# Hybrid GLA/NSA decoder layer on one core: 13 row sums in place of 18, full products for the top decay level, norm rows on ScalarE's queue

## Chip, cores and metric

The kernel runs on one core of a Trainium2 chip. The metric is the device time of one execution in microseconds. The time before is the median of three runs.

## The reference

One decoder layer for 256 tokens of width 2048, all in float32. `n = rms_norm(x)` goes through one input projection `w_in` (2048 x 5672). Four heads of gated linear attention (GLA) and eight query heads of a sparse attention (NSA: compressed, selected and window branches) read its parts. Both outputs go through `w_out` and are added to `x`. A SwiGLU network of inner width 5632 follows.

```python
h = x + concatenate([gla_out, nsa_out]) @ w_out
m = rms_norm(h, ffn_norm_g)
out = h + (silu(m @ w_gate) * (m @ w_up)) @ w_down
```

In GLA, the scores within a chunk are `sum_d q[t,d] k[s,d] exp(b[t,d] - b[s,d])` for `s <= t`, with `b` the running sum of a log gate.

## The kernel before

**Precision.** TensorE works on float32r numbers. Each operand is split into a high part (ScalarE: `hi`, L136, L623) and the rest (VectorE: `lo`, L137, L624), and a product is three matmuls: hi x hi, hi x lo, lo x hi, each 128x128 by 512 columns at most. Attention's small products are plain float32, which the profile shows as two matmul passes each.

**Stages.** `x` is turned (L209: transposes through the identity), scaled by the columns of `attn_norm_g` (L254, L256) and split. The gains come as 16 rows of 128 (L179) that a transpose turns into columns (L217, L218); L254 needs them. The ten projections (`proj`, L290; products at L282) follow each other, with weights loaded by 1 MB (L127) into three `raw` buffers on SP's queue. While they and the two halves of `w_out` run, `drive` (L97) hands out steps of attention from the queues `urgent` and `later`: `gla_decay`, `gla_scores`, `gla_out`, the NSA parts.

**GLA scores.** A 128x128 block of scores is put together from eight products, one for each level l of `LEVELS` (0, 1, 2, 4 ... 64). Level l gives the pairs (t, s) that lie in the two halves of one group of 2 l tokens. Seven of the eight products are full 128x128 ones (L567). At l = 64, where one quarter alone is wanted, the kernel multiplies 64 columns by 64 (L565). In both cases VectorE then copies that quarter alone (L574).

**Feed-forward in sevens.** The inner width is cut into 11 blocks f of 512 (`gate_up`, L1060). In each block the 2048 inputs are taken as 8 pairs of 128 rows, with 2 token tiles and the two matrices gate and up. Done plainly, a pair is 8 products of 128x128 by 512, that is 24 matmuls. Done by a seven-product scheme of Strassen's kind it is 7 products, 21 matmuls; these need four sums of token tiles (`forms`) and four sums of weight rows. The sums of weights are made on VectorE in the block itself (L1097 to L1099) and split as the weights are (ftwo<-g and ftwo<-fsum at L623 and L624); a pair in eight needs no sums. `FIRST7` says which pairs of block f go in seven: two in f = 0, four in f = 1, pairs 0 to 5 in f = 2 to 4, and all eight from `ALL7` = 5 on. `ORDER1` = (0,1,2,6,3,4,5,7) is the order of pairs for f below `ALL7`, `ORDER` = (0,...,7) from there on. After its last pair in seven, a block adds up the partial banks (L1125 to L1129). Then follows the down stage of the block before (96 matmuls at L282, weights `w_down` through L1040).

**Sums made ahead.** For some pairs, `sum_rows` (L1002) makes the four sums much earlier, while the projections run: it loads the pair's gate and up rows (two 512 KB requests on SP's queue, L1008), adds four times 128x512 on VectorE (L1013), and writes the two results to DRAM by GpSimd's queue (L1017). The block then loads one row of weights less and the sums (L1092), and VectorE makes none. `SUMS` lists these pairs: (2, 5, 7) for f = 5 to 10, 18 in all. They form the `background`: `drive` takes one step of it whenever `rate[0]` units of main work have gone by. The rates are 12, 30, 60, 18 and 14, in order of stage.

**Buffers.** In the feed-forward part weights go through three `fraw` buffers, split weights through four `ftwo`, sums through two `fsum`. SP's requests are issued in order, so one that waits for its buffer holds those behind it.

Of the kernel before, what the change touches and what calls it, by code (L numbers as in the profile page):

```python
# [15 lines left out]
P = 128  # L16
# [6 lines left out]
NFB = DFF // FB  # L23
# [13 lines left out]
def kernel(  # L37
# [4 lines left out]
    nc = tc.nc  # L42
    act, mm = nc.scalar.activation, nc.tensor.matmul
# [24 lines left out]
    def bank():  # L68
        n_tiles[0] += 1
        return pp.tile([P, 512], F32, tag="bank", name=f"bank_{n_tiles[0]}")  # L70

    def behind(op):

        return tc.issue_after(op.ins) if op is not None else nullcontext()
# [5 lines left out]
    urgent, later, background = [], [], []  # L80
# [11 lines left out]
    def drain(queue):  # L92
        while queue:
            for _ in queue.pop(0):
                pass
# [16 lines left out]
    count, rate = [0], [0]  # L112
# [55 lines left out]
    rows0, rows, rows2 = g1([P]), g1([P]), g1([P])  # L168
# [5 lines left out]
    for c in range(2):  # L174
        k = slice(2 * c, 2 * c + 2)
        nc.sync.dma_start(x_sb[0][:, :, c * 256:(c + 1) * 256], xv[:, :, c * 256:(c + 1) * 256])
        if c == 0:

            nc.sync.dma_start(rows0[0:16, :], attn_norm_g.rearrange("o (c p) -> (o c) p", p=P))  # L179
            for i in range(2):  # L180
                nc.scalar.dma_start(first[0][:, i], wi[i * P:(i + 1) * P, C_LR:C_LR + W0])
        else:
            nc.sync.dma_start(first[0][:, k], wi[2 * P:4 * P, C_LR:C_LR + W0].rearrange("(k p) w -> p k w", p=P))
# [308 lines left out]
    def ev_conv(ct, dst):  # L492
        def f(banks):
            urgent.append(conv(scaled(banks), ct, dst))
        return f

    def to_qk(dst):
        def f(pair, y):
            act(dst[:, 2 * pair:2 * pair + 2, :], y, AF.Silu)
            yield  # L500
        return f
# [54 lines left out]
    def gla_scores(h, b, res):  # L556
        tb = slice(b * P, (b + 1) * P)
        sc, e = g1([P]), dec[h // 2]
        for half in range(2):
            p = bank()  # L560
            for j in range(4):
                l = LEVELS[4 * half + j]
                u, w = (e[l][:, h % 2, tb],) * 2 if l else (kT[:, h, tb], qT[:, h, tb])
                if 2 * l == P:
                    mm(p[:l, j * P + l:(j + 1) * P], u[:, :l], w[:, l:], start=True, stop=True)  # L565
                else:
                    mm(p[:, j * P:(j + 1) * P], u, w, start=True, stop=True)  # L567
                yield
            for j in range(4):
                l, pl = LEVELS[4 * half + j], p[:, j * P:(j + 1) * P]  # L570
                if l == 0:
                    TT(sc, pl, lmask[:, 0, :], ALU.mult)
                elif 2 * l == P:
                    nc.vector.tensor_copy(sc[:l, l:], pl[:l, l:])  # L574
                else:
                    nc.vector.copy_predicated(sc, lmask[:, 4 * half + j, :].bitcast(mybir.dt.uint32), pl)
        res["s"] = sc
# [355 lines left out]
    PAIRS7, FIRST7 = tuple(range(8)), {0: (0, 2), 1: (0, 2, 4, 5)}  # L933

    EARLY7 = (0,1,2,3,4,5)

    ALL7 = 5
    FIRST7.update({f: (0,1,2,3,4,5) for f in range(2, ALL7)})


    OLD = (1, 3)
# [54 lines left out]
                pair_forms(2 * n + pair, v)  # L996


    SUMS = (2,5,7)
    row_sums = {}  # L1000

    def sum_rows(f, pair):  # L1002

        n_tiles[0] += 1
        gate, up = g4([2, 512]), g4([2, 512])
        for to, m in ((gate, w_gate), (up, w_up)):
            with behind(last["dma"]):
                nc.sync.dma_start(to, m[0][2 * pair * P:(2 * pair + 2) * P, f * FB:(f + 1) * FB].rearrange("(k p) w -> p k w", p=P))  # L1008
        for _ in range(3):
            yield True  # L1010
        for o, i in ((up[:, 0], up[:, 1]), (up[:, 1], gate[:, 1]), (gate[:, 1], up[:, 0]), (gate[:, 0], gate[:, 1])):
            with behind(last["d"]):
                TT(o, o, i, ALU.add)  # L1013
            yield True
        to = row_sums[f, pair] = [dp.tile([P, 2, 512], F32, name=f"sums{i}_{f}_{pair}") for i in range(2)]
        for part, a in zip(to, (up, gate)):
            nc.gpsimd.dma_start(part, a)  # L1017
        for _ in range(1):
            yield True
# [40 lines left out]
    def gate_up(fb):  # L1060
# [11 lines left out]

        order, sevens = (ORDER0, ORDER1, ORDER)[0 if fb == 0 else 1 if fb < ALL7 else 2], FIRST7.get(fb, PAIRS7)
        last7 = max(sevens, key=order.index)
# [117 lines left out]

    drive([proj(C_LR, ev_go(0), ((0, 256), (256, 272)), first_chunk)], 2)
    constants()
    background += [sum_rows(f, pair) for f in range(ALL7, NFB) for pair in SUMS]
    rate[0] = 12
    drive([proj(C_GO + 512, ev_go(1)), proj(0, ev_conv(0, to_qk(qT))), proj(512, ev_conv(4, to_qk(kT))),
           proj(1024, ev_conv(8, to_v(0))), proj(1536, ev_conv(12, to_v(1)))], 1.5)
    later.append(gla_mix())
    rate[0] = 30  # L1200
    drive([proj(C_KC, ev_kc), proj(C_KS, ev_kv(0)),
           proj(C_KW, ev_kv(1), ((0, 256), (256, 280))), proj(C_NQ, ev_nq(0))], 2.5)
    later.append(nsa_mix())
    rate[0] = 60
    drive([proj(C_NQ + 512, ev_nq(1))], 2.5)
    rate[0] = 18
    drive([w_out_half(0)], 2)
    drain(urgent)
    drain(later)
    rate[0] = 14  # L1210
    drive([w_out_half(1)], 6)

    for f in range(NFB):
# [39 lines left out]
```

## Time and profile before

| | |
|---|---|
| time, median of 3 runs | 1118.97 us (1118.44 to 1119.41) |
| profiled execution | 1119.94 us, its span 1118.2 us |
| instructions | 14700 |
| VectorE / ScalarE busy | 87% / 66% of the span |
| HBM read / written | 243.45 MB / 20.97 MB |

The span is what the trace covers of one execution. PE is TensorE's matmuls and PEld its weight loads, which overlap with PE; DVE is VectorE, ACT ScalarE, POOL GpSimd, SP the engine that issues most DMA requests. Names of tiles come without their numbers, so that `g` stands for many buffers. L1066 holds the products of `gate_up`, L282 those of projections, `w_out` and the down stages. Matmuls are pipelined: a busy time of PE counts the stretch from the first start to the last end, and the pace is read from the distance of starts.

### The profile page before, as it was taken

Reading aid. Unit: us, or ns where it says so; the run is one execution under the profiler, and the core shown is the slowest. Engines: PE = TensorE matmul, PEld = TensorE weight load, DVE = VectorE, ACT = ScalarE, POOL = GpSimd, SP = SyncE. Lnnn points to the kernel's source line nnn. Section 1 sums busy time; section 2 is a strip of 40 time slices with the busy share of each in tenths; the row PEclk is TensorE's granted clock in tenths of the full one; section 3 lists DMA queues with packets and bytes.
Section 4 is the critical chain, followed back from the end, with each engine's and each line's share of the span. In section 5 each row is a group of like instructions: output and inputs, shape, how many; then the busy total and the mean of one; then the engine's idle time right before and its main releaser. Section 6 shows DMA issues by size and latency. Waiting matters only on the chain.

```text
span 1118.2 us, 14700 instructions
## 1 busy us (share of the span) xinstructions
PE 1107.2 (99%) x5360; PEld 909.4 (81%) x5360; DVE 975.4 (87%) x1262; ACT 739.9 (66%) x1005; POOL 50.1 (4%) x97
## 2 busy tenths in 40 slices
PE   9999999999999999999999999999999999999998
PEld 8888887898778887887888888888878888888886
DVE  6678779988588889999899999899999999999981
ACT  6645557544575486657586676768686876868693
POOL 3110000111001001000000000000000000000000
PEclk9999999999999999999999999999999999999999
DMA  8999985475884686747465756767767768777772
GB/s 282 325 337 364 356 286 178 122 249 181 267 302 165 245 291 232 249 162 243 153 212 176 244 166 215 241 231 245 235 245 243 256 209 282 252 247 230 243 241 94
DMA packets 128338, 265.39 MB, mean 237 GB/s; under 512 B 6869, under 2 KB 9977, under 8 KB 128266
## 3 DMA queue, kind: packets, MB, share of 16 engines
q1 hardware_dynamic: 122794, 245.04, 64.8%
q0 software_dynamic: 5184, 18.88, 4.2%
q8 instruction: 42, 0.69, 0.2%
q10 hardware_dynamic: 288, 0.54, 0.2%
q14 instruction: 30, 0.25, 0.1%
HBM read 243.45 MB, written 20.97 MB: 236 GB/s over the span
## 4 chain that ended last, share of the span: by engine, by line
PE 90%; DVE 3%; DMA 3%; ACT 2%; issue 1%; POOL 0%; SPq 0%; ACTq 0%; POOLq 0%; DVEq 0%
PE bank L282 47%; PE bank L1066 36%; PE bank L209 3%; DMA raw<-in_w_out_dram 1%; PE bank L883 1%; PE bank L567 1%; DMA fraw<-in_w_down_dram 1%; DVE ftwo L624 1%; DVE lo L137 1%; ACT ftwo L623 1%; PE bank L821 1%; ACT hi L136 0%; DMA g<-in_attn_norm_g_dram 0%; PE bank L737 0%; POOL sm L212 0%
## 5 line engine op out<-in xcount | busy, mean ns | idle before, releaser
L1066 PE MATMUL bank<-ftwo,g 128*128 128x512 f32 x1848 | 431.6, 393 | 0.2 <-ACT ftwo L623 0.2
L1066 PEld LDWEIGHTS bank<-ftwo,g 128*128 128x128 f32 x1848 | 341.9, 188 | 77.1 <-DVE ftwo L624 3.1
L282 PE MATMUL bank<-hi,g 128*128 128x512 f32 (+2 forms) x1088 | 323.8, 377 | 0.0
L624 DVE TENSOR_TENSOR ftwo<-fraw,ftwo 128x1536 fp32r<-128x1536 f32 (+1 forms) x130 | 258.0, 1992 | 10.9 <-ACT ftwo L623 9.9
L282 PE MATMUL bank<-ftwo,g 128*128 128x512 f32 x1056 | 243.1, 390 | 0.7 <-ACT g L623 0.6
L623 ACT ACTIVATE ftwo<-fraw 128x1536 fp32r<-128x1536 f32 (+1 forms) x130 | 217.6, 1677 | 25.8 <-DMA fraw<-in_w_up_dram 13.5
L282 PEld LDWEIGHTS bank<-ftwo,g 128*128 128x128 f32 x1056 | 197.6, 188 | 43.4 <-ACT bank L1172 1.2
L282 PEld LDWEIGHTS bank<-hi,g 128*128 128x128 f32 x1088 | 192.8, 189 | 30.4 <-issue 1.0
L136 ACT ACTIVATE hi<-raw 128x1024 fp32r<-128x1024 f32 (+3 forms) x124 | 130.2, 1057 | 106.5 <-PE bank L282 64.6
L282 PE MATMUL bank<-lo,g 128*128 128x512 f32 (+3 forms) x544 | 195.3, 377 | 1.6 <-DVE lo L137 1.6
L137 DVE TENSOR_TENSOR lo<-raw,hi 128x1024 fp32r<-128x1024 f32 (+3 forms) x124 | 150.1, 1218 | 37.6 <-ACT hi L136 36.9
L623 ACT ACTIVATE ftwo<-g 128x1024 fp32r<-128x1024 f32 x72 | 76.2, 1059 | 75.2 <-DVE g L1097 59.8
L282 PEld LDWEIGHTS bank<-lo,g 128*128 128x128 f32 x544 | 98.7, 189 | 17.1 <-DVE lo L137 2.6
L624 DVE TENSOR_TENSOR ftwo<-g,ftwo 128x1024 fp32r<-128x1024 f32 x72 | 87.8, 1220 | 15.7 <-ACT ftwo L623 15.7
L1186 ACT COPY g<-bank 128x512 f32<-128x512 f32 (+1 forms) x96 | 51.4, 553 | 56.2 <-PE bank L282 54.1
L624 DVE TENSOR_TENSOR ftwo<-fsum,ftwo 128x1024 fp32r<-128x1024 f32 x72 | 87.8, 1220 | 0.4
L623 ACT ACTIVATE ftwo<-fsum 128x1024 fp32r<-128x1024 f32 x72 | 75.7, 1052 | 3.5 <-DVE fsum L1099 2.7
L1097 DVE TENSOR_TENSOR g<-fraw 128x1024 f32<-128x1024 f32 x54 | 65.3, 1219 | 0.3 <-issue 0.3
L1172 ACT COPY bank<-g 128x512 f32<-128x512 f32 x88 | 49.8, 593 | 12.4 <-DVE f L1128 10.7
L623 ACT ACTIVATE g<-bank 128x512 fp32r<-128x512 f32 (+1 forms) x50 | 29.0, 592 | 32.6 <-PE bank L209 22.2
L209 PE MATMUL bank<-ident,g 128*128 128x128 f32 (+2 forms) x214 | 37.5, 276 | 1.6 <-DMA g<-in_attn_norm_g_dram 1.3
L1099 DVE TENSOR_TENSOR fsum<-fsum,fraw 128x512 f32<-128x512 f32 x54 | 37.2, 689 | 0.8
(214 smaller groups left out, 812.1 us busy)
## 6 DMA issues: line engine op xcount, KB each, us to landing
fraw<-in_w_down_dram SPq DMA_DIRECT2D x44, 1024.0 KB, 5.0
fraw<-in_w_gate_dram SPq DMA_DIRECT2D x86, 512.0 KB, 3.9
raw<-in_w_in_dram SPq DMA_DIRECT2D x36, 1024.0 KB, 7.1
fraw<-in_w_up_dram SPq DMA_DIRECT2D x68, 512.0 KB, 4.9
sums<-g POOLq DMA_DIRECT2D x36, 512.0 KB, 6.4
raw<-in_w_out_dram SPq DMA_DIRECT2D x16, 1024.0 KB, 6.0
g<-in_w_gate_dram SPq DMA_DIRECT2D x18, 512.0 KB, 7.8
g<-in_w_up_dram SPq DMA_DIRECT2D x18, 512.0 KB, 8.1
```

The source lines that it names most:

```text
L136: act(h[:, i:i + n], r[:, k + i:k + i + n], AF.Copy)
L137: last["d"] = TT(o[:, i:i + n], r[:, k + i:k + i + n], f32(h[:, i:i + n]), ALU.subtract)
L209: return nc.tensor.transpose(o, i, ident[:n, :n])
L282: last["mm"] = mm(bk[t], a[:, k, t * P:(t + 1) * P], m[:, off:off + w], start=(first_ and k == 0 and i == 0), stop=(end and k == 3 and i = ...
L567: mm(p[:, j * P:(j + 1) * P], u, w, start=True, stop=True)
L623: act(hi, ps, AF.Copy)
L624: last["d"] = TT(lo, ps, f32(hi), ALU.subtract)
L1066: mm(banks[q], x, m, start=todo[q] == total[q], stop=todo[q] == 1)
L1097: TT(s1, r[:, 1:3], r[:, 3:4].to_broadcast([P, 2, 512]), ALU.add)
L1099: TT(s2[:, 1], s2[:, 0], r[:, 0], ALU.add)
L1172: nc.scalar.copy(banks[qs[n][t]], h_sb[n][:, t, :])
L1186: nc.scalar.copy(h_sb[n][:, t, cs], bs[t][:, cs])
```

## The change

Four edits:

- The blocks. `ALL7` goes from 5 to 9. Blocks 2 to 8 do pairs 0 to 5 and 7 in seven, and pair 6 in eight; blocks 9 and 10 do all in seven. So blocks 2 to 4 have one more pair in seven and blocks 5 to 8 one less. Blocks 5 to 8 now take `ORDER1`, where pair 6 comes fourth.
- The sums made ahead. `SUMS` holds pair 7 alone for blocks 2 to 8, and (2, 5, 7) for blocks 9 and 10: 13 in all. The background's rates go to 14, 36, 60, 22 and 17.
- The product at l = 64 is a full one like the others; VectorE still copies the same quarter.
- The 16 rows of `attn_norm_g` are requested on ScalarE's queue, ahead of its two slices of `w_in`, and no more on SP's queue between two parts of `x`.

```diff
-            nc.sync.dma_start(rows0[0:16, :], attn_norm_g.rearrange("o (c p) -> (o c) p", p=P))
+            nc.scalar.dma_start(rows0[0:16, :], attn_norm_g.rearrange("o (c p) -> (o c) p", p=P))
             for i in range(2):
                 nc.scalar.dma_start(first[0][:, i], wi[i * P:(i + 1) * P, C_LR:C_LR + W0])
...
-                if 2 * l == P:
-                    mm(p[:l, j * P + l:(j + 1) * P], u[:, :l], w[:, l:], start=True, stop=True)
-                else:
-                    mm(p[:, j * P:(j + 1) * P], u, w, start=True, stop=True)
+                mm(p[:, j * P:(j + 1) * P], u, w, start=True, stop=True)
...
-    ALL7 = 5
-    FIRST7.update({f: (0,1,2,3,4,5) for f in range(2, ALL7)})
+    ALL7 = 9
+    FIRST7.update({f: (0, 1, 2, 3, 4, 5, 7) for f in range(2, ALL7)})
...
-    SUMS = (2,5,7)
+    SUMS = {f: (2, 5, 7) if f >= ALL7 else (7,) for f in range(2, NFB)}
...
-    background += [sum_rows(f, pair) for f in range(ALL7, NFB) for pair in SUMS]
-    rate[0] = 12
+    background += [sum_rows(f, pair) for f in sorted(SUMS) for pair in SUMS[f]]
+    rate[0] = 14
...
-    rate[0] = 30
+    rate[0] = 36
...
-    rate[0] = 18
+    rate[0] = 22
...
-    rate[0] = 14
+    rate[0] = 17
```

## Prediction

> **What bounds the kernel now.** I read the page first, then the windows (busy time of each engine by stage), then the waits of PE, then the chain in order of time.
>
> ```profile
> span 1118.2 us, 14700 instructions
> PE 1107.2 (99%) x5360; PEld 909.4 (81%) x5360; DVE 975.4 (87%) x1262; ACT 739.9 (66%) x1005; POOL 50.1 (4%) x97
> DMA packets 128338, 265.39 MB, mean 237 GB/s; under 512 B 6869, under 2 KB 9977, under 8 KB 128266
> ```
>
> TensorE stands still for 1118.2 - 1107.2 = 11.0 us. So a gain has two sources only: fewer or quicker instructions on PE, or less of these 11 us. The windows of one feed-forward block before ALL7 (f = 3) and of two behind it (f = 6 and 7) show what a block costs; they are cut where the chain passes from one block's down stage to the next block. The columns after the stretch are its length, then busy us (instructions) of PE, PEld, DVE, ACT and POOL, the granted clock, the DMA share and GB/s.
>
> ```profile
> 598.68:661.13 62.45, 62.45 (x279) 51.17 (x279) 58.74 (x54) 43.02 (x45) 0.00 (x0) 1.00 0.61 202
> ...
> 784.79:846.40 61.61, 61.51 (x273) 49.87 (x273) 60.04 (x54) 45.81 (x49) 0.00 (x0) 1.00 0.71 243
> 846.40:907.63 61.23, 61.23 (x273) 49.99 (x273) 59.86 (x54) 45.59 (x49) 0.00 (x0) 1.00 0.72 245
> ```
>
> PE is busy throughout, so a block lasts as long as its products. Six pairs in seven and two in eight make 6 x 21 + 2 x 24 = 174 products (f = 2, 3, 4); eight in seven make 168 (f from 5). But DVE is close behind: 58.74 of 62.45 us, and 59.86 of 61.23. PE's real halts are few:
>
> ```profile
> PE bank L209 <- DMA g<-in_attn_norm_g_dram: 1.3, 1, 1.3
> ...
> PE bank L1066 <- DVE lo L137: 1.0, 1, 1.0
> ...
> PE bank L282 <- ACT g L623: 0.6, 1, 0.6
> ```
>
> Columns: total us, times, longest. Two of these lie where the change cuts: the wait for the norm rows at the start, and one wait for DVE where w_out ends and the first block begins.
>
> **1. Blocks in seven.** Before, the blocks hold 2 + 4 + 3 x 6 + 6 x 8 = 72 pairs in seven; after, 2 + 4 + 7 x 7 + 2 x 8 = 71, so 3 more products. A product's price is in the chain: the down stage inside block f = 4 is 96 of them.
>
> ```profile
> 701.83 21.76 PE bank L282 x96
> ```
>
> 21.76 / 96 = 0.227 us, so a pair in seven saves 3 x 0.227 = 0.68. f = 2, 3, 4 gain 0.68 each (-2.04), f = 5 to 8 lose 0.68 each (+2.72): together +0.68. By the windows, six products are 62.45 - 61.23 = 1.22, which makes it +0.61. I take **+0.6**, bounds +0.5 and +0.7, if DVE lets it. Its work in a block is worked out from f = 3's groups (count | busy us, mean ns | idle before):
>
> ```profile
> L624 DVE TENSOR_TENSOR ftwo<-fraw,ftwo 128x2048 fp32r<-128x2048 f32 x6 | 13.6, 2287 | 0.0
> L624 DVE TENSOR_TENSOR ftwo<-fraw,ftwo 128x1536 fp32r<-128x1536 f32 x6 | 10.5, 1754 | 0.0
> L624 DVE TENSOR_TENSOR ftwo<-g,ftwo 128x1024 fp32r<-128x1024 f32 x6 | 7.3, 1221 | 2.6 <-ACT ftwo L623 2.6
> L624 DVE TENSOR_TENSOR ftwo<-fsum,ftwo 128x1024 fp32r<-128x1024 f32 x6 | 7.3, 1220 | 0.1
> L1097 DVE TENSOR_TENSOR g<-fraw 128x1024 f32<-128x1024 f32 x6 | 7.1, 1219 | 0.0
> L1098 DVE TENSOR_TENSOR fsum<-g,fraw 128x512 f32<-128x512 f32 x6 | 4.1, 686 | 0.0
> L1099 DVE TENSOR_TENSOR fsum<-fsum,fraw 128x512 f32<-128x512 f32 x6 | 4.1, 686 | 0.0
> ```
>
> A pair in eight costs DVE 2.29; a pair in seven with ready sums 1.75 + 1.22 + 1.22 = 4.19; one without, 4.19 + 1.22 + 0.69 + 0.69 = 6.79. After, blocks 2 to 8 hold six pairs of 6.79, one of 4.19, one of 2.29: f = 3's 58.74 + 4.19 - 2.29 = 60.64, in 62.45 - 0.68 = 61.77 us. That leaves 1.13 us, against 1.37 in f = 7, which runs with no halt of PE. And the lag is the same: while PE does a pair in seven (4.77 us) DVE falls behind by 2.02 in a pair of 6.79 and wins 0.58 in one of 4.19. f = 7 has five and three: 5 x 2.02 - 3 x 0.58 = 8.4. After: 6 x 2.02 - 0.58 - (5.45 - 2.29) = 8.4. Both end with a pair of 6.79 and then a ready one, so the requests of w_down on SP's queue, held by the release of fraw, come equally late. The two last blocks do not change.
>
> **2. Fewer sums in the background.** 18 - 13 = 5 fewer; each is 4 additions (L1013), 1 MB read, 1 MB written, and later 1 MB of sums read in place of 0.25 MB of weights: 2.75 MB x 5 = 14 of 265 MB. Most of that hides under PE, which is busy there, and is worth nothing. One place is on the path. A sum takes 9 steps of the background, so 162 before and 117 after. The drives count 2 units for a product group: 960 in the first five projections, 768 in the next four, 192 in the last, 384 in each half of w_out. At the old rates they offer 960/12 + 768/30 + 192/60 + 384/18 + 384/14 = 157 steps up to the end of w_out; at the new ones (17 acts as 18) 69 + 21 + 3 + 17 + 21 = 131. So before, the additions run into the first block; after, they end in the first quarter of w_out's second half, and the built order of DVE's instructions agrees. Here is the chain at that end:
>
> ```profile
> 420.74 0.68 DVE g L1013
> ...
> 422.03 0.60 DVE g L1013
> ...
> 427.79 1.15 DVE lo L137
> ...
> 428.97 1.20 PE bank L1066 x4
> ```
>
> Two additions, 1.28 us, stand in the chain ahead of PE's 1.0 us wait. Without them DVE's part is there 1.28 us sooner and the wait goes; between these rows DVE runs without a pause, so it is not held by ACT. **-1.0**, bounds 0 and -1.3. What is late next is PE's own work. The 0.6 us wait at the first down stage hangs on DVE too, which carries four more additions after 429 us before: I count half, **-0.3** (0 to -0.6). f = 6 lasts 61.61 for its neighbours' 61.23, and with DMA at 0.6 in place of 0.7 I count **-0.2** (0 to -0.4). I give nothing for the two halts for w_out (0.57 and 0.71 us), whose requests are held by raw buffers, not by the background.
>
> ```profile
> 297.38 0.51 PE L282 MATMUL bank<-lo,g 128*128 128x512 f32 x1 [0.57 <-DVE lo L137]
> 305.98 0.50 PE L282 MATMUL bank<-lo,g 128*128 128x512 f32 x1 [0.71 <-DVE lo L137]
> ```
>
> **3. Top scores.** Eight products (two passes each) go from 64 x 64 to 128 x 128. PE's timeline has both kinds between w_in's products; the first column is the start:
>
> ```profile
> 257.95 0.48 PE L282 MATMUL bank<-lo,g 128*128 128x512 f32 x1
> 258.27 0.38 PE L567 MATMUL bank<-g 128*128 128x128 f32 x2
> 258.41 0.48 PE L282 MATMUL bank<-hi,g 128*128 128x512 f32 x1
> 258.81 0.33 PE L565 MATMUL bank<-g 128*64 128x64 f32 x2
> 259.07 0.50 PE L282 MATMUL bank<-hi,g 128*128 128x512 f32 x1
> ```
>
> A full one (L567) lets its neighbour start 0.14 later, and the round from L282 to L282 is 0.46. The narrow one holds its neighbour for 0.26 and itself starts 0.08 later: 0.66. So the half-size product is 0.20 dearer at this place and, by its 0.26 against 0.14, at least 0.12 everywhere: 8 x 0.16 = **-1.3**, bounds 0 (if DVE ends that stretch) and -1.6. The Trainium skill ("TensorE: Matmul & The Clock Gate", Back-to-back issue gap) gives a matmul of up to 64 columns some 60 cycles and one of 128 columns 134, by which this term would be about +0.5, an estimate, in place of -1.3. This trace does not agree: 0.26 us against 0.14. Another page of the Trainium skill ("TensorEngine Tiling (Array Packing)", Key Properties) sides with the trace: a change of tiling mode drains the engine.
>
> **4. Norm rows.** From the timeline of the first microseconds:
>
> ```profile
> 0.80 0.91 ACTq L181 DMA_DIRECT2D raw<-in_w_in_dram  x2
> 1.25 2.93 PE L199 MATMUL bank<-g 128*128 128x256 f32 x6 [1.25 <-DVE g L193]
> 1.31 0.45 SPq L179 DMA_DIRECT2D g<-in_attn_norm_g_dram  x1
> 5.47 1.30 PE L209 MATMUL bank<-ident,g 16*128 16x16 f32 x5 [1.29 <-DMA g<-in_attn_norm_g_dram]
> 7.18 0.63 ACT L322 ACTIVATE hi<-raw 128x528 fp32r<-128x528 f32 x1
> ```
>
> The rows are asked for at 1.31, behind x on SP's queue, and PE waits for them until 5.47. On ACT's queue they are asked for at 0.80: with the same time to land, 0.5 sooner. The other end is the whole 1.29, when x has landed by 4.18, PE's last filler; x was there at 5.66 at the latest, when its transposes followed. I take **-0.7**. ACT's two slices of w_in go 0.45 later; the first is used at 7.18, so it has room, and SP's eight loads behind the rows go 0.5 sooner. No DMA wait is seen on PE behind this, so the gain is kept.
>
> **Sum.** +0.6 - 1.0 - 0.3 - 0.2 - 1.3 - 0.7 = -2.9. The profiled execution took 1119.94 us (span 1118.2), 0.97 over the median of the other runs, so the terms are put on the median: 1118.97 - 2.9 = **1116.1**.
>
> **Rivals.**
> - The halts only move: terms 2 and 4 come to nothing since another engine ends the same stretch (ACT at 429, x at the start). Then +0.6 - 1.3 = -0.7: 1118.3. For it: DVE is at 68.8 of 72 us just after 429. Against: two additions stand in the chain itself.
> - The narrow products are the cheaper ones after all, and their 0.26 and 0.08 are chance of the place. With half the columns such a product would hold its neighbour for 0.07 in place of L567's 0.14, and term 3 would be +8 x 0.07 = +0.6: -2.9 + 1.3 + 0.6 = -1.0, or 1118.0. The rows above speak against it. This is the Trainium skill's rule of the issue gap, named in part 3.
> - Slower: DVE becomes the bound in blocks 2 to 8. Three pairs of 6.79 now follow each other (3, 4, 5), where f = 7 has at most two. If the lead won in pair 6 is lost because ftwo has only four buffers, the third pair's lag of 2.02 shows at the first product of w_down, which in f = 7 had little to spare:
>
> ```profile
> 883.05 2.28 DVE L624 TENSOR_TENSOR ftwo<-fraw,ftwo 128x2048 fp32r<-128x2048 f32 x1
> 885.62 2.68 PE L282 MATMUL bank<-ftwo,g 128*128 128x512 f32 x11
> ```
>
>   DVE is done at 885.33, the lo part is used at 885.85: 0.5 us. So up to 1.5 us a block, seven times: 1116.1 + 10.5 = 1126.6. It decides the sign from 2.9 / 7 = 0.41 us a block on.
> - The move of the rows does not do what it says: x, not the rows, is what lands last, term 4 is nothing, and it is 1116.8. The chain names the rows, but a wait for several is put down to the last.
> - More: the two halts for w_out go as well, since less is read beside them: 1116.1 - 1.3 = 1114.8.
>
> **How the numbers follow.** About 0.2% (2.2 us) is what a measurement of this kernel can tell from no change. Forecast 0.46, and without term 4, which is x in the rows' place, 0.05. More: 0.10. The halts only move: 0.18. The narrow products cheaper: 0.04. DVE the bound: 0.17, of which 0.03 stays within 0.2%. Faster by over 0.2% takes the forecast and More, and 0.04 of the case without term 4: 0.60; within it 0.26; slower 0.14. The lower ends of all terms give +0.5 - 1.3 - 0.6 - 0.4 - 1.6 - 1.3 = -4.7, or 1114.3, and with the halts for w_out 1113.0; the range begins half-way, at 1113.6. It ends at 1120.0, the rival of DVE at 0.56 us a block; beyond stand its dearer forms, 0.14.
>
> **What would show it.** PE's first L209 begins before 5.0 us. No L565 of 64 columns is left, and each round with a top score is 0.46. No L1013 after 400 us, and no wait of PE at 429. Windows of f = 2 to 8 near 61.8 us, DVE near 60.6. I am wrong if PE waits for ftwo in these blocks, or if they differ from 61.8 by over 0.3 us.

## Result and the profile after

The changed kernel takes **1124.33 us** (median of 16 runs, 1119.79 to 1131.75), the kernel before 1119.32 (16 runs on the same chip, 1118.44 to 1120.45). The ratio is 1.0044, 95% interval 1.0035 to 1.0054: it is **slower by 5.0 us**, where the prediction said 2.9 us faster and gave 1120.0 as the upper end. The runs also lie further apart: 12 us, against 2.

The profiled execution took 1126.33 us. Lines of the changed kernel have other numbers from L567 on: mostly three less, so L1066, L1092, L623, L624, L1013, L1097 to L1099 and L1172 are now L1063, L1089, L620, L621, L1010, L1094 to L1096 and L1169. The head of its page:

```profile
span 1124.6 us, 14618 instructions
PE 1108.9 (99%) x5363; PEld 911.1 (81%) x5363; DVE 970.8 (86%) x1256; ACT 745.0 (66%) x1003; POOL 43.4 (4%) x87
DMA packets 123378, 250.97 MB, mean 223 GB/s; under 512 B 6389, under 2 KB 9497, under 8 KB 123306
```

What the edits were to remove is removed: 14 MB less moved, 4.6 us less on DVE, three products more on PE. But TensorE's idle time went from 11.0 to 1124.6 - 1108.9 = 15.7 us. The waits of PE say on whom (total us, times, longest):

```profile
PE bank L1063 <- ACT ftwo L620: 4.5, 4, 2.1
PE bank L282 <- ACT bank L1169: 1.8, 2, 1.2
...
PE bank L209 <- DVE g L782: 0.9, 1, 0.9
PE bank L209 <- ACT g L976: 0.8, 1, 0.8
PE bank L767 <- ACT g L746: 0.6, 1, 0.6
```

The waits for the norm rows (1.3) and for `lo` at 429 us (1.0) are gone, as forecast. All but 0.2 us of the first two rows is new and lies in blocks 2 to 8; the last three lie between 297 and 392 us. The windows of blocks 4 to 7, cut as in the prediction, show where the time went:

```profile
657.97:719.99 62.02, 62.02 (x276) 50.64 (x275) 60.52 (x57) 44.95 (x48) 0.00 (x0) 1.00 0.61 216
719.99:785.33 65.34, 63.58 (x276) 51.79 (x275) 60.62 (x57) 45.20 (x48) 0.00 (x0) 0.97 0.59 205
785.33:849.40 64.07, 61.95 (x276) 50.64 (x275) 60.15 (x57) 45.18 (x48) 0.00 (x0) 1.00 0.60 209
849.40:911.27 61.87, 61.87 (x276) 50.64 (x275) 60.72 (x58) 45.17 (x48) 0.00 (x0) 1.00 0.63 215
```

Blocks 4 and 7 (first and last row) take 62.02 and 61.87 us, close to the 61.8 of the prediction, with DVE at its 60.6. The others of blocks 2 to 8 have the same program and take up to 65.34. DVE is no busier in a long block than in a short one. So the forecast holds for a block that runs through, and most do not. Together blocks 2 to 8 take 441.8 us, against 432.6 before. The balance of the profiled executions: block 2 begins 3.2 us earlier (532.9 for 536.1), blocks 2 to 8 take 9.2 more, the rest 0.4 more: +6.4, which is 1124.6 - 1118.2.

Here is the worst block, the second row, in the chain in order of time, and SP's requests of the same stretch:

```profile
744.74 1.14 DVE ftwo L621
745.88 0.61 DVE fsum L1096
...
746.50 8.04 DMA fraw<-in_w_down_dram
...
754.63 2.87 ACT ftwo L620 x2
...
757.54 6.20 PE bank L1063 x19
```

```profile
745.90 0.34 SPq L1089 DMA_DIRECT2D g<-sums  x1
746.50 0.38 SPq L1037 DMA_DIRECT2D fraw<-in_w_down_dram  x1
749.31 0.33 SPq L1089 DMA_DIRECT2D fsum<-sums  x1
751.65 2.05 SPq L1037 DMA_DIRECT2D fraw<-in_w_down_dram  x2
```

The first load of `w_down` (1 MB) takes the `fraw` buffer of the third pair from the end. That is pair 4, which makes its own sums, so the buffer is free only when its last addition (L1096) ends, at 746.49, 26.5 us into the block. The sums of pair 7 (two loads of 512 KB) are asked for at 745.90 and 749.31. So 2 MB are asked for within 3.4 us. On ACT the split of `w_down` stands ahead of the split of the second sum; both wait for their data, and PE's last pair waits for ACT:

```profile
754.63 1.91 ACT L620 ACTIVATE ftwo<-fraw 128x2048 fp32r<-128x2048 f32 x1 [1.91 <-DMA fraw<-in_w_down_dram]
756.45 1.04 ACT L620 ACTIVATE ftwo<-fsum 128x1024 fp32r<-128x1024 f32 x1
```

Before, blocks 2 to 4 asked for `w_down` as late, but had no sums to load. Blocks 5 to 8 had sums, and there the third pair from the end (5) was a ready one. Here are the same requests in block 5 of the kernel before, which begins at 723.43, and ACT's split of `w_down`:

```profile
746.39 0.38 SPq L1040 DMA_DIRECT2D fraw<-in_w_down_dram  x1
748.67 0.33 SPq L1092 DMA_DIRECT2D g<-sums  x1
749.80 0.33 SPq L1092 DMA_DIRECT2D fsum<-sums  x1
```

```profile
757.88 1.91 ACT L623 ACTIVATE ftwo<-fraw 128x2048 fp32r<-128x2048 f32 x1
```

So there, too, 2 MB were asked for within 3.4 us, and they landed after 5.1, 4.5 and 4.6 us. But `w_down` was asked for 23.0 us into the block, landed at 28.1, and ACT came to it at 34.4: 6.4 us to spare. In the changed block ACT has done all else at 32.7, so a landing may take 6.2 us; a landing of 5.0 leaves about 1 us, and this one took 8.0. The next two loads of `w_down` also follow closer: the two sums and the first three loads of `w_down`, 4 MB, are asked for within 7.4 us here and within 10.5 before. The second load of `w_down` can be late in the same way: in block 2 it is asked for at 31.6 us and takes 7.3, and the 0.6 us halt of the second row of waits follows.

After the halt PE had half its clock for 3.4 us. The two groups of 13 products on either side of it, from PE's timeline, and the window behind it, with the clock 0.50:

```profile
752.64 3.14 PE L1063 MATMUL bank<-ftwo,g 128*128 128x512 f32 x13
757.54 4.84 PE L1063 MATMUL bank<-ftwo,g 128*128 128x512 f32 x13 [1.76 <-ACT ftwo L620]
```

```profile
757.84:761.24 3.40, 3.40 (x9) 2.67 (x8) 3.15 (x3) 2.65 (x3) 0.00 (x0) 0.50 0.60 228
```

The same 13 products take 1.70 us more; this is the 0.97 in the clock's column. So a wait of 1.76 us cost 3.5. The 2.1 us wait in block 6 was longer and cost no clock (1.00 in its row). Of the 9.2 us, the halts of the first two rows in these blocks are 6.1, the clock is 1.7 and the three more products, which were forecast, 0.6; the rest lies in shorter delays. The Trainium skill ("TensorE: Matmul & The Clock Gate", Part 1) says that the clock is halved after an idle window of some 3.4 us which runs freely, and comes back after as long a busy one. That it hits one halt and not another fits a free-running window; that 1.76 us of halt are enough does not fit the 3.4 us.

### The profile page after: what moved, and what is told of

Same layout as the page of the kernel before. It is cut to its first block, busy times and chain, and to the rows that moved or that the text cites. A ratio compares the mean times of both kernels' runs of the same rounds, so it can differ in the third digit from the quotient of the medians.

```text
span 1124.6 us, 14618 instructions
## 1 busy us (share of the span) xinstructions
PE 1108.9 (99%) x5363; PEld 911.1 (81%) x5363; DVE 970.8 (86%) x1256; ACT 745.0 (66%) x1003; POOL 43.4 (4%) x87
## 4 chain that ended last, share of the span: by engine, by line
PE 73%; DVE 12%; issue 6%; DMA 4%; ACT 3%; POOL 0%; ACTq 0%; SPq 0%; POOLq 0%; DVEq 0%
PE bank L282 45%; PE bank L1063 23%; DVE ftwo L621 7%; PE bank L209 2%; ACT ftwo L620 2%; DVE g L1094 2%; DMA fraw<-in_w_down_dram 1%; DMA raw<-in_w_out_dram 1%; PE bank L880 1%; DVE fsum L1096 1%; DVE fsum L1095 1%; DMA g<-in_w_up_dram 1%; PE bank L818 1%; PE bank L564 1%; DMA fsum<-sums 1%
## 5 line engine op out<-in xcount | busy, mean ns | idle before, releaser
L1063 PE MATMUL bank<-ftwo,g 128*128 128x512 f32 x1851 | 434.6, 394 | 4.5 <-ACT ftwo L620 4.5
L1063 PEld LDWEIGHTS bank<-ftwo,g 128*128 128x128 f32 x1851 | 344.2, 188 | 82.1 <-ACT ftwo L620 7.3
L282 PE MATMUL bank<-hi,g 128*128 128x512 f32 (+1 forms) x1088 | 326.0, 377 | 0.3 <-ACT hi L322 0.3
L621 DVE TENSOR_TENSOR ftwo<-fraw,ftwo 128x1536 fp32r<-128x1536 f32 (+1 forms) x130 | 259.0, 1995 | 17.8 <-ACT ftwo L620 17.3
L620 ACT ACTIVATE ftwo<-fraw 128x1536 fp32r<-128x1536 f32 (+1 forms) x130 | 218.5, 1681 | 38.3 <-DMA fraw<-in_w_up_dram 23.5
L620 ACT ACTIVATE ftwo<-g 128x1024 fp32r<-128x1024 f32 x71 | 75.1, 1058 | 61.4 <-DVE g L1094 30.1
L621 DVE TENSOR_TENSOR ftwo<-g,ftwo 128x1024 fp32r<-128x1024 f32 x71 | 86.6, 1220 | 9.4 <-ACT ftwo L620 9.4
L621 DVE TENSOR_TENSOR ftwo<-fsum,ftwo 128x1024 fp32r<-128x1024 f32 x71 | 86.6, 1219 | 5.0 <-ACT ftwo L620 4.8
L620 ACT ACTIVATE ftwo<-fsum 128x1024 fp32r<-128x1024 f32 x71 | 74.6, 1051 | 7.6 <-DVE fsum L1096 5.7
L1094 DVE TENSOR_TENSOR g<-fraw 128x1024 f32<-128x1024 f32 x58 | 69.5, 1218 | 0.0
L1169 ACT COPY bank<-g 128x512 f32<-128x512 f32 x88 | 49.8, 592 | 10.6 <-DVE f L1125 8.6
L620 ACT ACTIVATE g<-bank 128x512 fp32r<-128x512 f32 (+1 forms) x50 | 29.2, 592 | 37.7 <-PE bank L209 30.8
L1096 DVE TENSOR_TENSOR fsum<-fsum,fraw 128x512 f32<-128x512 f32 x58 | 39.8, 686 | 0.5
```

The lines of the kernel that those rows point to most:

```text
L282: last["mm"] = mm(bk[t], a[:, k, t * P:(t + 1) * P], m[:, off:off + w], start=(first_ and k == 0 and i == 0), stop=(end and k == 3 and i = ...
L620: act(hi, ps, AF.Copy)
L621: last["d"] = TT(lo, ps, f32(hi), ALU.subtract)
L1063: mm(banks[q], x, m, start=todo[q] == total[q], stop=todo[q] == 1)
L1094: TT(s1, r[:, 1:3], r[:, 3:4].to_broadcast([P, 2, 512]), ALU.add)
L1096: TT(s2[:, 1], s2[:, 0], r[:, 0], ALU.add)
```

## Experiments

In each profile, the start of block 2 gives what happened ahead of it, and the sum of blocks 2 to 8 what happened in them. The ratio is to the kernel before on the same chip in the same stretch of time. A letter in an expectation names a theory that is stated there.

| kernel | median (range) us | ratio, 95% interval | span | block 2 starts | blocks 2 to 8 |
|---|---|---|---|---|---|
| before | 1119.32 (1118.44 to 1120.45) | 1 | 1118.2 | 536.1 | 432.6 |
| after | 1124.33 (1119.79 to 1131.75) | 1.0044 (1.0035 to 1.0054) | 1124.6 | 532.9 | 441.8 |
| e1 start and scores alone | 1116.99 (1115.80 to 1117.98) | 0.998 (0.9971 to 0.9989) | 1116.2 | 532.5 | 432.6 |
| e2 blocks, sums, rates alone | 1127.04 (1124.57 to 1127.20) | 1.0062 (1.0046 to 1.0077) | 1125.3 | 536.5 | 439.1 |
| e3 no loads of sums | 1118.31 (1117.50 to 1119.57) | 0.9994 (0.9985 to 1.0003) | 1116.5 | 533.6 | 433.0 |
| e4 order, pair 6 last | 1133.95 (1133.36 to 1134.78) | 1.0131 (1.0117 to 1.0144) | 1133.1 | 535.2 | 447.9 |
| e5 two ready pairs | 1121.82 (1119.90 to 1124.82) | 1.003 (1.0019 to 1.004) | 1120.7 | 537.4 | 432.7 |
| e6 old rates | 1119.37 (1117.34 to 1122.42) | 1.0 (0.999 to 1.0009) | 1120.7 | 532.0 | 439.0 |
| e7 sums on GpSimd's queue | 1121.32 (1118.64 to 1122.65) | 1.0017 (1.0008 to 1.0026) | 1119.7 | 533.5 | 436.6 |
| e8 e1 with two rates quicker | 1118.26 (1117.23 to 1121.84) | 1.0001 (0.9992 to 1.001) | 1118.4 | 534.7 | 432.2 |
| e9 after, unaltered | 1124.55 (1120.62 to 1126.49) | 1.0042 (1.0028 to 1.0056) | 1124.8 | 534.0 | 441.1 |
| e10 order, pair 6 third from the end | 1138.29 (1134.68 to 1140.05) | 1.0169 (1.0153 to 1.0185) | 1135.4 | 532.8 | 452.3 |
| e11 e10 with old rates | 1137.30 (1136.88 to 1140.21) | 1.017 (1.0156 to 1.0183) | 1135.2 | 532.0 | 452.1 |
| e12 old rates again | 1119.69 (1117.46 to 1124.13) | 1.0012 (1.0 to 1.0024) | 1115.8 | 531.1 | 433.8 |
| e13 first two rates old | 1121.03 (1116.27 to 1125.16) | 1.0019 (1.0006 to 1.0033) | 1114.5 | 531.4 | 433.3 |
| e14 last two rates old | 1121.72 (1118.87 to 1124.68) | 1.0021 (1.0011 to 1.0031) | 1121.4 | 533.8 | 437.4 |
| e15 order, pair 7 third from the end, old rates | 1130.84 (1129.70 to 1132.35) | 1.0104 (1.0089 to 1.0119) | 1128.0 | 531.7 | 446.1 |
| e16 order, pair 7 second from the end, old rates | 1132.33 (1131.48 to 1133.89) | 1.0119 (1.0102 to 1.0135) | 1130.5 | 531.1 | 448.6 |

**The parts.** e1 is the kernel before with the two small edits:

```diff
-            nc.sync.dma_start(rows0[0:16, :], attn_norm_g.rearrange("o (c p) -> (o c) p", p=P))
+            nc.scalar.dma_start(rows0[0:16, :], attn_norm_g.rearrange("o (c p) -> (o c) p", p=P))
...
-                if 2 * l == P:
-                    mm(p[:l, j * P + l:(j + 1) * P], u[:, :l], w[:, l:], start=True, stop=True)
-                else:
-                    mm(p[:, j * P:(j + 1) * P], u, w, start=True, stop=True)
+                mm(p[:, j * P:(j + 1) * P], u, w, start=True, stop=True)
```

> The kernel before with two of the four edits: norm rows on ScalarE's queue and the full product at l = 64. Blocks, sums and rates as before. Theory A (all the loss is in blocks 2 to 8, where the first request of w_down comes 3.5 us later in a block than in blocks 5 to 8 before, because its buffer and its place on SP's queue hang on the third-last pair, which now makes its own sums): the trace of the changed kernel is 0.75 us ahead through the projections and about 1.4 more behind the scores, so 1119.3 - 0.75 - 1.4 = 1117.2, spread as small as before. Rival B (VectorE's load in the blocks is at its limit, and any shift of what comes before disturbs them): no gain, or over 1119.3.

Measured 1116.99, 2.3 us under the kernel before. e2 is the other half: the changed kernel with these two edits undone.

> The changed kernel with the other two edits undone: norm rows on SP's queue, narrow product at l = 64; blocks, sums and rates as changed. Theory A: 2.1 us over the changed kernel, 1126.4, with halts of PE of 0.5 to 2.5 us in some of blocks 2 to 8 about 35.4 us or 40.5 us after the block's first product, and a spread of several us. Rival C (the two small edits cost time themselves): under 1124.

Measured 1127.04. So the small edits gain 2.3 to 2.7 us and the blocks with their sums and rates lose 7 to 8; it is these that were misjudged.

**What halts the blocks: the loads, or VectorE's lag?** In e3, blocks 2 to 8 do not load pair 7's sums but split values that lie in SBUF; pair 7's true sums are thereby left out, and the two buffers for them are not taken. VectorE, ScalarE and TensorE do as much as in the changed kernel.

```diff
-                sums = s1, s2 = g4([2, 512]), (fw["sum"] if fw else g4)([2, 512])
-                for to, part in zip(sums, ready):
-                    nc.sync.dma_start(to, part)
+                sums = s1, s2 = (g4([2, 512]), (fw["sum"] if fw else g4)([2, 512])) if fb >= ALL7 else (None, None)
+                if fb < ALL7:
+                    s1, s2 = (f32(a).rearrange("p (a b) s -> p a (b s)", a=2) for a in (hT_h[0], hT_h[1]))
+                else:
+                    for to, part in zip(sums, ready):
+                        nc.sync.dma_start(to, part)
```

> The changed kernel, but blocks 2 to 8 do not load the sums of pair 7: the split reads other values that lie in SBUF, of the same size, so that part of the computation is left out (the sums of pair 7 are not those of the weights). VectorE, ScalarE and TensorE do the same work; two requests of 512 KB a block are gone from SP's queue, one just ahead of the first w_down and one right behind it. Theory A (late landings, of w_down and of the sums, hold ScalarE and through it the last pair): w_down lands some 2 us sooner, the halts at 35.4 us go, 1116 to 1118. Rival B (VectorE's load is the bound): VectorE has the same to do, the halts stay, over 1122.

Measured 1118.31, just above theory A's range and far below B's. The window of block 5:

```profile
719.78:781.47 61.69, 61.69 (x276) 50.71 (x275) 60.34 (x57) 44.88 (x48) 0.00 (x0) 1.00 0.60 201
```

DVE's 60.34 us fit into 61.69 and PE never stands. The seven blocks take 433.0 us, with one halt: in block 4 a load of gate and up rows landed late, VectorE began 0.9 us later, and PE waited 0.7 us for it. `w_down` is still asked for at 26.5 us in most blocks, and where the trace tells it landed after 5.0 to 5.2. So neither DVE's load nor the late request alone is the cause of the large halts; it takes the loads of the sums as well.

e4 tries another order in these blocks, with pair 6 last:

```diff
     ORDER1 = (0,1,2,6,3,4,5,7)
+    ORDER2 = (0,1,2,7,3,4,5,6)
...
```

> The changed kernel with the order 0,1,2,7,3,4,5,6 in blocks 2 to 8: pair 7 with its ready sums comes fourth, pair 6 in eight comes last. The loads on every engine are the same. Theory A: the last pair needs no sums and gives PE 5.4 us, so w_down's late landing holds nothing, and blocks last 61.8: 1116 to 1118. Rival B (VectorE's lag over three pairs that make their own sums decides): the lag before the last pair is larger by 2.6 us without the pair in eight in the middle, so halts move to pair 5 and the time is 1124 or more.

I was wrong about it: every block takes 63.9 to 64.0 us, and PE waits for VectorE, twice a block:

```profile
PE bank L1064 <- DVE ftwo L621: 7.3, 14, 0.8
```

This is the prediction's rival, the lag behind three own-sum pairs in a row, and it comes when the eight-product pair no longer stands ahead of them. It is the same in every block, and the runs lie 1.4 us apart. The changed kernel's large halts differ from block to block and are for ACT; they are another thing.

e5 has two ready pairs, 5 and 7, in blocks 2 to 8, so that a ready pair is third from the end; 20 sums in all, at rates 12, 24, 60, 16, 12.

```diff
+    ORDER2 = (0,1,2,6,3,5,4,7)
...
-    SUMS = {f: (2, 5, 7) if f >= ALL7 else (7,) for f in range(2, NFB)}
+    SUMS = {f: (2, 5, 7) if f >= ALL7 else (5, 7) for f in range(2, NFB)}
```

> The changed kernel, but blocks 2 to 8 have two ready pairs (5 and 7) and end ... 3, 5, 4, 7, so that the last three pairs are ready, own sums, ready, as in the blocks of the kernel before that ran without a halt. 20 sums, rates 12, 24, 60, 16, 12. Theory A: the first w_down is asked for 23 us into the block again, not at 26.5, the sums of the last pair at 26.4 and not 29.3, and the halts in blocks 2 to 8 go, so 8 us less than the changed kernel: 1116.5 to 1118.5, small spread. Rival D (a landing is slow here whenever sums are read beside w_down): blocks 2 to 8 keep halts of 0.5 to 2.5 us, 1121 or more.

The total missed the expectation, the blocks did not. `w_down` is asked for at 21 us of the block, no block has a halt, and they take 432.7 us together, twice as many loads of sums notwithstanding. VectorE has less to do here as well, 58.4 us a block for 60.6, so this run alone does not tell the two theories apart; e3 does. Block 3:

```profile
599.00:660.74 61.74, 61.74 (x276) 50.69 (x275) 58.36 (x53) 44.85 (x48) 0.00 (x0) 1.00 0.66 230
```

What it lost it lost ahead of block 2, which starts 4.5 us later than in the changed kernel: the additions of its 20 sums run on to 455.7 us, into the first two blocks, which take 112.2 us in place of 108.6, with a new wait of 2.1 us for ACT at 429.

e7 moves the loads of sums of blocks 2 to 8 to another queue.

```diff
-                    nc.sync.dma_start(to, part)
+                    (nc.gpsimd if fb < ALL7 else nc.sync).dma_start(to, part)
```

> The changed kernel, but blocks 2 to 8 request the ready sums on GpSimd's queue, which has nothing else to do there, in place of SP's. Theory A1 (order on SP's queue: w_down stands behind a request of the sums that waits for its buffer): w_down is asked for up to 3 us sooner, halts are halved: under 1121. Theory A2 (w_down waits for its own buffer until 26 us anyway, and both land slowly side by side): it is asked for at most 0.6 us sooner and the halts stay: 1122 to 1126.

It came out between the two. `w_down` is asked for at 26.5 as before, so SP's order does not hold it; it is the buffer. The blocks took 436.6 us, with halts of 0.7, 0.6 and 1.4 us in blocks 2, 4 and 7.

**The rates.** A rate is the number of units between two steps, so a smaller one is quicker. e6 is the changed kernel with the background's old rates; the prediction has no term for the rates by themselves.

```diff
-    rate[0] = 14
+    rate[0] = 12
...
-    rate[0] = 36
+    rate[0] = 30
...
-    rate[0] = 22
+    rate[0] = 18
...
-    rate[0] = 17
+    rate[0] = 14
```

> The changed kernel with the background's old rates 12, 30, 60, 18, 14: its 13 sums then end in the first half of w_out. In the front the changed kernel has three halts that the kernel before lacks (0.9 us at 297, 0.6 at 309, 0.8 at 391 us). Theory E: they come from where the background's additions fall on VectorE, so with other rates the one at 297 goes and the front is about 1 us shorter; the halts in blocks 2 to 8 stay: 1122.5 to 1124. Rival F: the halts hang on the blocks' edit alone and stay where they are: 1124.3 or more.

Both sides missed on the time: 1119.37, as fast as the kernel before. The halt at 297 us went and block 2 starts 0.9 us earlier, as theory E has it. e8 is e1 with the second and fourth rate made quicker (30 to 24, 18 to 16):

> The kernel before with norm rows on ScalarE's queue, the full product at l = 64, and rates 12, 24, 60, 16, 14, so that all 18 sums end before w_out does. Theory G (two additions of the background stand in the chain of the 1.0 us wait at the first block): that wait goes and the time is 1.0 us under the kernel with the two edits alone, 1116.0. Rival H (the steps that move into attention's stages delay it as much): 1117 or more.

Measured 1118.26: the quicker rates cost e1 1.3 us by the medians, and block 2 starts 2.2 us later. The wait at the first block does not go; it is now 1.2 us for ACT in place of 1.0 for VectorE, and waits of 0.8 us at 260 and 0.7 at 392 are new. Rival H holds. So e1, with the old rates, is the best kernel here. To tell luck from a lasting difference, the changed kernel was run once more, and e6 too, with its two halves (e13: the first two rates taken back, e14: the last two):

> The changed kernel once more, unaltered, beside the next two. If the 5 us between it and the kernel with the old rates (1119.4) are what the rates do, it stays at 1123.5 to 1125 with its blocks 2 to 8 at 440 us or more in all; if they are mostly the luck of how the transfers fell in one execution, its median moves under 1122 or its blocks sum to 437 or less, with halts in other blocks than before.

> The changed kernel with the old rates 12, 30, 60, 18, 14, once more, beside its two halves. If the 5 us to the changed kernel are lasting, its median is 1118.5 to 1120.5 again, with block 2 starting at 531.5 to 532.5; if they were the luck of that call, 1122 or more.

> The changed kernel with only the first two rates taken back, 14 to 12 and 36 to 30; those under the two halves of w_out stay 22 and 17. If the halts at 298 and 310 us come from the sums of rows that the rate of 36 puts among the work of the heads, they go, block 2 starts 0.9 to 1.5 us earlier than in the changed kernel, and the time falls to 1121 to 1123.5; if the rates act through w_out's halves, it stays at 1124 or more.

> The changed kernel with only the rates under the two halves of w_out taken back, 22 to 18 and 17 to 14. By the front's halts the time stays within 1 us of the changed kernel's 1124.4, and the halts at 298 and 310 us stay; if these rates decide (what is left of the background when the blocks begin), 1119 to 1121.

The two medians stay: 1124.55 and 1119.69. e13 took 1121.03, as forecast for the case that the first rates count; e14 took 1121.72, outside both of its ranges. So each half of the rates is worth some 3 of the 5 us. One part of the 5 us is clear. Here is VectorE in the changed kernel at 296 us, and PE behind it:

```profile
295.68 0.68 DVE L782 COPY g<-bank 128x512 f32<-128x512 f32 x1
...
296.40 0.68 DVE L1010 TENSOR_TENSOR g<-g,g 128x512 f32<-128x512 f32 x1
297.01 0.68 DVE L782 COPY g<-bank 128x512 f32<-128x512 f32 x1
```

```profile
297.75 0.33 PE L209 MATMUL bank<-ident,g 128*128 128x128 f32 x1 [0.94 <-DVE g L782]
```

An addition of the background (L1010) has come between two copies of attention's softmax (L782) on which PE's next transposes hang. In e13 the copies follow each other, and PE does not wait:

```profile
294.81 0.68 DVE L782 COPY g<-bank 128x512 f32<-128x512 f32 x1
...
295.53 0.69 DVE L782 COPY g<-bank 128x512 f32<-128x512 f32 x1
```

The waits for L782 and L746 are there in the changed kernel, e3, e7, e9 and e14, whose second rate is 36 (and in e2, three lines further down), and in none of e6, e12 and e13, where it is 30. Together they are 1.5 us. Block 2 starts at 532.9 to 534.0 us in the first group (leaving out e2, which lacks the two small edits) and at 531.1 to 532.0 in the second; e13 is 1.5 us ahead of the changed kernel. So the first two rates are worth 1 to 2 us here, and the halts that go with the second are as much. The 0.8 us wait for L976 at 392 us is there with old rates too; its cause is not shown.

The rest is in the blocks, whose program the rates do not touch. The profiled execution of e13 shows what the change could have given. Blocks 3 and 5 of it:

```profile
593.06:654.84 61.78, 61.78 (x276) 50.63 (x275) 60.42 (x57) 45.02 (x48) 0.00 (x0) 1.00 0.64 217
...
716.87:778.63 61.76, 61.76 (x276) 50.66 (x275) 60.40 (x57) 45.14 (x48) 0.00 (x0) 1.00 0.62 217
```

All seven take 61.7 to 62.2, and none has a halt of over 0.3 us; this execution took 1116.27 us, while others of the same kernel took up to 1125.16. Block 5 of it asks for the same data at the same times as block 5 of the changed kernel. Set side by side, the stretches from 3 to 8.6 us after the request of the first sum; the last column is GB/s. The changed kernel, then e13:

```profile
748.90:751.90 3.00, 3.00 (x14) 2.36 (x14) 3.00 (x5) 1.70 (x3) 0.00 (x0) 1.00 0.88 299
751.90:754.50 2.60, 2.60 (x13) 2.11 (x13) 2.60 (x3) 0.82 (x1) 0.00 (x0) 1.00 0.95 307
```

```profile
745.80:748.80 3.00, 3.00 (x15) 2.43 (x14) 3.00 (x5) 1.75 (x3) 0.00 (x0) 1.00 1.05 407
748.80:751.40 2.60, 2.60 (x13) 2.13 (x13) 2.60 (x3) 2.60 (x3) 0.00 (x0) 1.00 0.82 262
```

Over the first 3 us the same requests move at 299 GB/s in one execution and at 407 in the other. The DMA issues of these two blocks (last column: us from issue to landing) give, for the changed kernel and for e13:

```profile
fraw<-in_w_down_dram SPq DMA_DIRECT2D x1, 1024.0 KB, 8.0
...
fsum<-sums SPq DMA_DIRECT2D x1, 512.0 KB, 6.5
```

```profile
fraw<-in_w_down_dram SPq DMA_DIRECT2D x1, 1024.0 KB, 5.4
...
fsum<-sums SPq DMA_DIRECT2D x1, 512.0 KB, 3.8
```

By the 6.2 us that a landing may take, 5.4 passes and 8.0 is 1.8 too long: the halt. What slows the requests in one execution stays open, and with it why the changed kernel's rates bring late landings more often than the old ones (441.8 and 441.1 us of blocks in its two profiles; 439.0, 433.8, 433.3 and 437.4 with some or all of the rates old).

**Can the two loads be taken apart?** Three more orders of the pairs were tried. The first two runs put pair 6, in eight, third from the end.

```diff
+    ORDER2 = (0,1,2,3,4,6,5,7)
...
```

> The changed kernel with the order of the pairs in blocks 2 to 8 turned to 0, 1, 2, 3, 4, 6, 5, 7: the eight-product pair stands third from the end, so the first load of w_down takes the buffer of a pair that makes no sums. Theory A (the halts come from the late first load of w_down, which meets the two loads of sums): it is asked for at 21 to 24 us of the block and not at 26.5, lands in about 5 us, the halts at 35.4 and 40.5 us go, blocks last 61.6 to 62.0 us, their sum falls from 441.8 to 432 to 434 and the time to 1115 to 1117. Rival B (VectorE's lag behind the own sums decides, as in the kernel with the eight-product pair last): halts of 0.5 us and more in every block after pair 4, blocks of 62.5 us and more, 1120 or more.

> The same order with the old rates 12, 30, 60, 18, 14 of the background. If the old rates save what the front of the earlier kernel with them showed, block 2 starts 0.9 us earlier (at 532.0) and the time is 0.5 to 1.5 us below the kernel with the new order alone, 1114 to 1116 by theory A; if the rates matter only through the halts in the blocks, both give the same within 0.4 us.

Theory A failed here: both runs take 1.017 times the kernel before, the second with the old rates. VectorE falls behind pairs 3 and 4, which now follow each other without the eight-product pair ahead of them, and with it `w_down` is asked for no sooner (26.8 us). The largest of PE's waits in e10:

```profile
PE bank L1064 <- DVE ftwo L621: 4.7, 8, 0.6
```

The last two try pair 7 earlier, with old rates and with a product of raw weights first in the last pair:

```diff
+    ORDER2 = (0,1,2,6,3,7,4,5)
...
-                for q in (6, 1, 5, 7, 2, 3, 4) if at == 7 else (1, 2, 3, 5, 7, 6, 4):
+                for q in (6, 1, 5, 7, 2, 3, 4) if at == 7 and (ready or fb < 2) else (1, 6, 5, 7, 2, 3, 4) if at == 7 else (1, 2, 3, 5, 7, 6, 4):
...
```

> The changed kernel with the old rates and the order 0, 1, 2, 6, 3, 7, 4, 5 in blocks 2 to 8: the ready pair stands third from the end, so the first load of w_down takes the buffer of a pair that makes no sums, and the loads of sums come before it; pair 5, which makes its own sums, is last (its first product is one of raw weights). Theory A (late w_down and sums beside it make the halts): w_down is asked for at 20 to 24 us of the block, the sums earlier still, no halt over 0.5 us but perhaps at the last pair, blocks of 61.7 us, 432 to 433.5 in all, 1114 to 1117 with a spread of under 3 us. Rival B (VectorE's lag): with a pair of own sums last, PE waits for VectorE in every block, 0.3 us or more, 1119 or more with a small spread.

```diff
+    ORDER2 = (0,1,2,6,3,4,7,5)
...
```

> The same with the order 0, 1, 2, 6, 3, 4, 7, 5: pair 4, which makes its own sums, is still third from the end, so w_down is asked for as late as in the changed kernel (26 us or more), but the sums of pair 7 are asked for some 5 us earlier than there. If it is the meeting of the two that costs, the halts at 35.4 go and the time is 1115 to 1118; if the late w_down alone is enough, the halts at 40.5 us stay in most blocks and it is 1119 to 1122.

In e15 `w_down` is asked for at 20.7 us, the sums at 11 and 15; its loads of `w_down` land in 5.0 us by the median, as they did before. The first of a block still takes 7.1 to 7.7 us where the trace tells, but ACT comes to it at 34.5 or later, over 6 us after it has landed. The irregular halts are gone but for one of 0.7 us, and its four runs lie 2.7 us apart. But a pair that makes its own sums is last, and VectorE is late for it: every block takes 63.5 to 64.1 us, and PE waits 0.6 in each. e15's DMA issues and the largest of PE's waits:

```profile
fraw<-in_w_down_dram SPq DMA_DIRECT2D x44, 1024.0 KB, 5.0
```

```profile
PE bank L1064 <- DVE ftwo L621: 4.1, 7, 0.6
```

e16 shows the same loss, and `w_down` was asked for at 24.4 us and not at 26 or later, so it cannot tell whether the sums alone matter. With one ready pair in these blocks, I found no order that has both: either `w_down` comes late beside the sums, or VectorE is late. Not tried was to split the second sum on ACT ahead of `w_down`.

## Why the prediction was wrong, point by point

- **Norm rows, -0.7.** Right. The rows are asked for at 0.81 and PE's first transposes follow their filler with no wait:

```profile
0.81 0.46 ACTq L179 DMA_DIRECT2D g<-in_attn_norm_g_dram  x1
...
4.11 1.33 PE L209 MATMUL bank<-ident,g 16*128 16x16 f32 x5
```

  Through the first projections the products run 0.5 to 1.0 us earlier than before, for the most part 0.75, and e1's 0.7 to 0.9. The rivals that put x in the rows' place fall.

- **Top scores, -1.3.** Right in mechanism; the gain is 1.8, a little beyond the bound of 1.6. From the timelines of the kernel before and of e1, set side by side at the products of `w_in`, seven of the eight rounds gain 0.14 to 0.22 us; the eighth, where other products stand between, 0.35. The rule of the Trainium skill ("TensorE: Matmul & The Clock Gate", Back-to-back issue gap), by which a narrow product is cheaper, does not hold here. e1 gains some 0.7 more in this stretch, 0.5 of it at 219 us, where a wait of the kernel before for `lo` (0.30) goes.
- **Fewer sums, -1.0 and -0.3.** Right where it was looked for: no L1010 after 381 us, no wait at 429, and blocks 0 and 1 take 108.6 us for 109.9. But the prediction asked only which additions go, not where the new rates put those that stay. Those cost 1.5 us at 298 and 310 us by e13. So at the start of block 2, 0.5 to 1.4 us of the 1.3 are there with the old rates (531.1 to 532.0 us in e6, e12 and e13, for 532.5 in e1, which has all 18 sums), and nothing with the new ones (532.9 and 534.0). The list of what the change adds had the rates in it only as a count of steps.
- **Block 6, -0.2.** Not borne out. In e13's run without halts block 6 is the longest of the seven (62.2 us); in e3, which loads no sums in these blocks, it is as long as its neighbours (61.7).
- **Blocks in seven, +0.6.** This is the step that failed: "Both end with a pair of 6.79 and then a ready one, so the requests of w_down on SP's queue, held by the release of fraw, come equally late." The last two pairs are alike, but the buffer is that of the third from the end. There the old blocks 5 to 8 have a ready pair, and the changed blocks one that makes its own sums: 23.0 against 26.5 us. Of the 6.4 us that `w_down` had to spare on ACT, about 1 was left. That is harmless alone (e3, and blocks 2 to 4 before). With the loads of sums beside it the first load took 5.3 to 8.0 us to land in place of 5.0, and +0.6 became +9.2 (+8.5 in e9). That `w_down` and the sums come within 3.4 us of each other is not new and not enough; why they land late in some blocks and not in others stays open. That the term itself was right is shown by e3 and by e13's execution: +0.4 and +0.7.
- **The slower rival.** Its number (up to 1126.6) came near, its mechanism did not: PE's large waits in the changed blocks are not for VectorE, and e3 runs with the same load on VectorE. The lag is real, though. e4, e10, e15 and e16, each with one ready pair, show it, at 2 to 3 us a block over the 61.7 of e3, as soon as the pairs stand otherwise. The order of the changed kernel just escapes it, but for block 4: there PE waits 0.3 to 0.9 us for VectorE in six of the traces with this order (e3, e6, e7, e9, e12, e14). The prediction asked what VectorE would do with little time to spare at the first product of `w_down`, and not what a load 3.5 us later would.
- **The chances.** 0.14 for slower left out the case that decided. The range's upper end of 1120.0 is about the fastest run of the changed kernel.

## What to carry to other kernels

When the order of work changes, follow each buffer in the ring to the one who frees it, for every load behind: it is not the neighbour in the list that holds a load, but the user of its buffer some places earlier. Then ask how long the load may take until its first reader is free, for the old order and for the new one. Here 6.4 us to spare became about 1, and with transfers close by whose landing varies that turned into halts that differ from run to run, so the spread of the times belongs to the result.

Background work that is handed out by a counter is not free: another rate moves each of its pieces, and a 0.7 us addition between two links of a chain is a 0.9 us halt. Of the edits here, the two small ones alone make the better kernel: 1116.99 us, 0.998 of the kernel before (0.9971 to 0.9989).

## What the runs showed of the hardware

- A halt of 1.76 us on TensorE was followed by 3.4 us at a granted clock of 0.50 (13 products in 4.84 us for 3.14), one of 2.1 us in the same execution was not. Halts of 1.95 us in e14 and 2.27 in e9 were followed by it too, one of 2.10 in e2 was not. The added 1.7 us are as much as the halt itself.
- The same loads, asked for at the same times of the block, moved at 299 GB/s over 3 us in one execution and at 407 in another; the 1 MB load landed after 8.0 us in the one and 5.4 in the other. Without the sums beside it, in e3, it was 5.0 to 5.2.
- A 64-column product between full ones cost 0.14 to 0.22 us more than a 128-column one in its place, seven times out of eight; the eighth time it was 0.35, with other products between.
